# Pinning some weight loads to their place in the program on one DMA queue of a hybrid encoder block

## The chip, the cores and the metric

One core of a Trainium2 chip runs the whole kernel. Its engines are TensorE (PE in the profile, matmuls), VectorE (DVE, elementwise), ScalarE (ACT, elementwise and functions), GpSimd (POOL, elementwise) and SyncE (SP), which here does nothing but issue DMA transfers; each engine runs its own instructions in order and waits on semaphores for the others. The metric is the device time of one execution in microseconds, lower is better.

## The reference

A residual block on x of 512 frames by 1024 features, in float32:

```python
xn = rmsnorm(h, norm_mix_g[l])
u = jnp.einsum('bsd,de->bse', xn, w_in[l])
q, k, v, xr, gr, ga, gb = jnp.split(u, splits, axis=-1)
ya = chunked_band_attention(q, k, v, rel_table[l]) @ w_attn_out[l]      # 16 heads of 64
xc = causal_depthwise_conv(xr, conv_w[l], conv_b[l])
hr = rg_lru(xc, w_rg_r[l], b_rg_r[l], w_rg_i[l], b_rg_i[l], rg_lambda[l])
yb = (hr * jax.nn.gelu(gr)) @ w_rnn_out[l]
gates = jax.nn.sigmoid(jnp.concatenate([ga, gb], axis=-1) + b_merge[l])
g_a, g_b = jnp.split(gates, 2, axis=-1)
h = h + (g_a * ya + g_b * yb) @ w_o[l]
hn = rmsnorm(h, norm_ffn_g[l])
g, up = jnp.split(hn @ w_ffn_in[l], 2, axis=-1)
h = h + (jax.nn.silu(g) * up) @ w_ffn_out[l]
out = rmsnorm(h, final_norm_g)
```

## The kernel before

**Arithmetic.** Every product is made of three matmuls at reduced precision: both operands are split into a high part (ScalarE, line 82, rounds it) and a low part (VectorE, line 83, subtracts). A weight so split is a tile `whl_...`, from a loaded tile `raw_...` (line 143, issued by SP). For some large products (v, w_o, w_ffn_in, w_ffn_out) the kernel saves matmuls by Strassen-like sums of weight blocks. These sums of weights are made early, in time that VectorE has left over, and kept in DRAM: `spill` loads four blocks of 128 x 1024 (line 599, SP), makes four differences on VectorE (line 603), each in place, and stores each (lines 605 and 607, SP) into `sums...`, from where they are read much later. `spill_in` does the same for the first unit of w_ffn_in (loads at line 625, four operations at 628 to 632, stores at 635).

**Stages.** The recurrent branch comes first (xr, gr, gb; tiles u, gt, a, rnn), then the products `po_yb` of `rnn` with w_rnn_out, then v (`pv_mm`), then 16 attention heads, then the outputs, w_o and the FFN, which takes over half of the time.

**Where the loads stand in the program.**
- w_o: in the loop of the eight `po_yb` products, ahead of numbers 1 and 3, `spill_of(w_o, ...)` with four loads each (tiles `spillo0_n`, `spillo1_n`).
- w_ffn_out, unit 0 (tiles `spill_a2`, `spill_a3`, two loads each), and w_ffn_in (tiles `spill_fg2`, then `spill_fu2`, two loads each, in the same room): the generator `spills()`, which the loop of heads advances by one step ahead of each head from 2 on.

Around that loop a head h is worked thus: `transposed(h)` turns the probabilities `p` on TensorE (`pT`, line 744) and splits them (`pp`); `scores(h + 1)` makes `s` on TensorE from q, kh and kl (lines 725 and 726), the row maximum on VectorE (729), the exponential on ScalarE (730), the reciprocal `rl` of its sum on VectorE (731) and the normalisation on GpSimd (733); then come projections of q and k of a later pair of heads (`po_q`, `po_k`) and `weigh(h)` (`o`, line 764). q is copied out by ScalarE (678) and VectorE (679); kh and kl of a pair of heads by ScalarE (689, 691), VectorE (690) and GpSimd (692): kl of the odd head is GpSimd's copy of VectorE's difference.

**What sets the order.** On TensorE the program's order, by `manual_schedule`, in the heads and in the products of v. On SP, VectorE, ScalarE and GpSimd a scheduler orders the instructions of the program when the kernel is built, by its own model of when each can start, within their data dependencies and the room in the pools: so a load may be issued ahead of loads that stand in front of it in the program, and an operation on a loaded tile may stand ahead of others.

Of the kernel before, what the change touches and what calls it, by code (L numbers as in the profile page):

```python
# [14 lines left out]
P = 128  # L15
D = 1024
S = 512
# [15 lines left out]
CW = 256  # L33
# [3 lines left out]
def block_kernel(ctx: ExitStack, tc: tile.TileContext, x, norm_mix_g, w_in, b_merge, rel_table,  # L37
# [3 lines left out]
    pe, dve, act, pool, sp = nc.tensor, nc.vector, nc.scalar, nc.gpsimd, nc.sync  # L41
# [82 lines left out]
    units = (2, 3), (4, 5), (6, 7), (8, 9), (1, 10)  # L124
# [413 lines left out]
    def big(n, shape, dtype, name):  # L538
        return rnp.tile(shape, dtype, tag=f"big{n}", bufs=1, name=name)
# [42 lines left out]
    def drams(name):  # L582
        return [dr.tile([P, 2, S], F32, name=f"{name}_{n}") for n in range(4)]

    sums_d = [drams(f"sums{u}") for u in range(len(units))]
# [3 lines left out]
    def square(w, i, cc):  # L589
        rows = w[2 * P * i:2 * P * (i + 1), cc * S:(cc + 1) * S]  # L590
        return rows.rearrange("(k p) e -> p k e", p=P)
# [1 line left out]
    def fo_block(i, cc):  # L593
        return square(w_ffn_out, i, cc)

    def spill(w, unit, to, r):

        for n in range(4):
            sp.dma_start(out=r[n], in_=square(w, unit[n // 2], n % 2))
        b11, b12, b21, b22 = r  # L600
        for out_, i, a_, b_ in ((b11, 0, b12, b11), (b12, 2, b22, b12), (b22, 1, b22, b11), (b21, 3, b21, b22)):
            yield
            dve.tensor_sub(out_, a_, b_)
            if out_ is not b11:
                sp.dma_start(out=to[i][:], in_=out_)
            if out_ is b22:
                sp.dma_start(out=to[0][:], in_=b11)
# [5 lines left out]
    def spill_of(w, u, pl, tag, bufs):  # L613
        name, unit, to = {id(w_v): ("v", units_v, sums_v), id(w_o): ("o", units_o, sums_o)}.get(id(w), ("f", units, sums_d))
        r = [pl.tile([P, 2, S], F32, tag=tag, bufs=bufs, name=f"spill{name}{u}_{n}")[:] for n in range(4)]
        return spill(w, unit[u], to[u], r)

    first_sums = {f"f{w}2": [dr.tile([P, 2, 4, P], F32, name=f"sums_f{w}2_{n}") for n in range(2)] for w in "gu"}

    def spill_in(name, both):  # L620

        col = chunks[index[name]][1][0][1]
        r = [both[:, n] for n in range(2)]
        for n in range(2):
            sp.dma_start(out=r[n], in_=w_ffn_in[n * S:(n + 1) * S, col:col + CW].rearrange("(k p) e -> p k e", p=P))
        s2, s3, s4, s1 = (r[n][:, :, i * P:(i + 1) * P] for n in range(2) for i in range(2))
        yield
        dve.tensor_add(s1, s3, s1)
        dve.tensor_sub(s3, s2, s3)
        yield  # L630
        dve.tensor_sub(s2, s1, s2)
        dve.tensor_sub(s4, s4, s2)
        for to, of in zip(first_sums[name], ((s2, s1), (s3, s4))):
            for i in range(2):
                sp.dma_start(out=to[:, i], in_=of[i])
# [8 lines left out]
    for j in range(0, KT, 2):  # L644
        if j >= 4:
            at_once(spill_of(w_v, j // 2 - 2, early, "spill", 4))
        for c in range(2):
            conv[j + c] = rnn_conv(j + c, tile_of(f"xr{j}", c, ahead=2))
        for c in range(2):
            po = tile_of(f"gr{j}", c, "mm" if j == 0 else "t")  # L650
            conv[j + c] += (rnn_gelu(j + c, po),)
            gates_of(j + c)
        for c in range(2):
            gate(1, j + c)
# [221 lines left out]
    for j in range(KT):  # L876
        if j in (1, 3):
            at_once(spill_of(w_o, j // 2, aw, "v", 8))
        if j in (4, 5, 6, 7):
            xv_sum(("s1", "s2", "s4", "s3")[j - 4])  # L880
        if j == 6:
            blocks_v("b11")
        if j == 7:
            blocks_v("b21")
        po = mm_tile(f"po_yb{j}")
        project(po, weights(f"yb{j - j % 2}", 1 if j < 6 else 0), j % 2, rnn)
        dve.scalar_tensor_tensor(zB[j], zB[j], 1.0, po[:], ALU.add, ALU.mult)
# [37 lines left out]

    def spills():
        r = [big(n, [P, 2, 2, S], F32, f"spill_a{n}") for n in (2, 3)]
        yield from spill(w_ffn_out, units[0], sums_d[0], [r[n // 2][:, n % 2] for n in range(4)])
        yield from spill_in("fg2", big(2, [P, 2, 4, CW], F32, "spill_fg2"))
        yield from spill_in("fu2", big(3, [P, 2, 4, CW], F32, "spill_fu2"))  # L930

    spilling = spills()

    with tc.manual_schedule(engines={mybir.EngineType.PE}):
# [307 lines left out]
    def late():  # L1242
        for u in (1, 2, 3):
            yield from spill_of(w_ffn_out, u, acp, "act", 13)
# [26 lines left out]
    for j in range(2, FT, 2):  # L1271
# [6 lines left out]
        g, u = (sc.tile([P, 4, 256], F32, tag=f"c{w}", name=f"c_{w}{j}") for w in "gu")  # L1278
# [143 lines left out]
    with tc.manual_schedule(engines={mybir.EngineType.PE, mybir.EngineType.DVE, mybir.EngineType.Activation}):  # L1422
# [44 lines left out]
        x, w = acts["a22", last[0]], parts_w["t4", last[0]]  # L1467
# [39 lines left out]
```

## Time and profile before

| | us |
|---|---|
| median of 3 runs | 864.84 (864.70 to 865.08) |
| the profiled execution | 864.55 |
| its span, first to last instruction | 862.7 |
| TensorE busy | 845.0 (98%) |
| VectorE busy | 678.7 (79%) |
| ScalarE busy | 521.0 (60%) |
| GpSimd busy | 117.0 (14%) |
| mean granted TensorE clock | 0.995 of full speed |

Times in the profile's rows count from the first instruction. A row of a timeline gives start, duration, engine, line, operation, tiles (output<-inputs, numbers left out), shape, how many in a row, and in brackets how long the engine was idle before it and what released it. Engines with a q at the end (SPq) are the sequencers that issue transfers. The execution has 1.85 us around the span.

### The profile page before, as it was taken

The numbers are of one execution on the slowest core, as the hardware profiler recorded it, in microseconds if no ns is written. First come the engines' busy times: TensorE is split into PE (matmuls) and PEld (weight loads), VectorE is DVE, ScalarE is ACT, GpSimd is POOL, SyncE is SP. The second block draws the span as 40 slices with busy tenths as digits, with TensorE's granted clock in tenths as the row PEclk, the third lists the DMA queues.
The fourth block names the chain that finished last, engine by engine and source line by source line (L and its number), as shares of the span: only waits on it lengthen the run. The fifth ranks groups of instructions, "written<-read, shape, count | busy, mean of one in ns | idle before, by whom it ended". The sixth has DMA issues, their size and how long they took to land.

```text
span 862.7 us, 13109 instructions
## 1 busy us (share of the span) xinstructions
PE 845.0 (98%) x4860; PEld 738.7 (86%) x4860; DVE 678.7 (79%) x1006; ACT 521.0 (60%) x893; POOL 117.0 (14%) x152
## 2 busy tenths in 40 slices
PE   8999999999998999999999999999999999999997
PEld 6977887788886888888888889999999999988885
DVE  5789767797687777665568887988989887689985
ACT  7678677624565676766655456655565555385455
POOL 2324302220012433232200000000000001000002
PEclk9999999999998999999999999999999999999999
DMA  8694333953699422323247451565666242886622
GB/s 273 198 311 152 98 98 95 366 198 122 190 307 290 128 74 74 101 84 96 75 149 242 147 194 50 160 235 163 256 205 228 85 126 91 278 300 208 209 73 98
DMA packets 107599, 147.23 MB, mean 171 GB/s; under 512 B 7184, under 2 KB 77440, under 8 KB 107536
## 3 DMA queue, kind: packets, MB, share of 16 engines
q1 hardware_dynamic: 103856, 138.74, 48.9%
q10 hardware_dynamic: 3680, 7.67, 2.9%
q8 instruction: 38, 0.62, 0.3%
q14 instruction: 25, 0.20, 0.1%
HBM read 123.27 MB, written 23.11 MB: 170 GB/s over the span
## 4 chain that ended last, share of the span: by engine, by line
PE 85%; DVE 5%; DMA 3%; ACT 3%; POOL 2%; issue 1%; SPq 0%; ACTq 0%; DVEq 0%; POOLq 0%
PE po_out L76 4%; PE po_out L78 4%; PE po_out L77 4%; PE p_fu L76 2%; PE p_fg L78 2%; PE p_fu L78 2%; PE p_fu L77 2%; PE p_fg L76 2%; PE p_fg L77 2%; PE o L764 2%; PE po_ga L76 2%; PE po_ga L78 2%; PE po_ya L76 2%; PE po_ga L77 2%; PE po_ya L78 2%; PE po_ya L77 2%
## 5 line engine op out<-in xcount | busy, mean ns | idle before, releaser
L733 POOL TENSOR_SCALAR p<-p,rl 128x128 f32<-128x128 f32 (+1 forms) x64 | 41.6, 668 | 104.5 <-DVE rl L731 104.4
L730 ACT ACTIVATE p<-p,m 128x128 f32<-128x128 f32 (+1 forms) x64 | 35.8, 563 | 11.2 <-DVE m L729 11.2
L1219 POOL TENSOR_TENSOR act_lo<-act,act_hi 128x1024 fp32r<-128x1024 f32 x1 | 2.4, 2407 | 294.3 <-ACT act_hi L1218 294.3
L83 DVE TENSOR_TENSOR pp<-pT,pp 128x384 fp32r<-128x384 f32 (+1 forms) x48 | 28.0, 597 | 11.1 <-ACT pp L82 10.9
L83 DVE TENSOR_TENSOR whl_t<-raw_t,whl_t 128x1024 fp32r<-128x1024 f32 x26 | 32.1, 1236 | 0.3 <-ACT whl_t L82 0.3
L729 DVE CUSTOM_DVE_ANT_0 p<-s,bias 128x128 f32<-128x128 f32 (+1 forms) x64 | 29.0, 483 | 1.9 <-PE s L726 1.7
L76 PE MATMUL po_gr<-xnT,whl_gr 128*128 128x512 f32 (+1 forms) x80 | 28.2, 354 | 0.1
L82 ACT ACTIVATE whl_t<-raw_t 128x1024 fp32r<-128x1024 f32 x26 | 27.2, 1047 | 1.5 <-PE po_h L78 1.5
L77 PE MATMUL po_xr<-xnT,whl_xr 128*128 128x512 f32 (+1 forms) x80 | 27.8, 353 | 0.1
L77 PE MATMUL po_gr<-xnT,whl_gr 128*128 128x512 f32 (+1 forms) x80 | 27.6, 346 | 0.0
L78 PE MATMUL po_gr<-xnT,whl_gr 128*128 128x512 f32 (+1 forms) x80 | 27.5, 348 | 0.0
L78 PE MATMUL po_xr<-xnT,whl_xr 128*128 128x512 f32 (+1 forms) x80 | 27.3, 346 | 0.0
L76 PE MATMUL po_xr<-xnT,whl_xr 128*128 128x512 f32 (+1 forms) x80 | 26.7, 352 | 0.6 <-ACT xnT L358 0.6
L83 DVE TENSOR_TENSOR whl_fg_s<-s_fg,whl_fg_s 128x1024 fp32r<-128x1024 f32 x20 | 24.4, 1223 | 2.9 <-ACT whl_fg_s L82 2.9
L83 DVE TENSOR_TENSOR whl_fu_s<-s_fu,whl_fu_s 128x1024 fp32r<-128x1024 f32 x20 | 24.4, 1223 | 2.9 <-ACT whl_fu_s L82 2.9
L77 PE MATMUL po_yb<-rnn,whl_yb 128*128 128x512 f32 x64 | 25.1, 392 | 1.2 <-POOL rnn L549 1.2
L83 DVE TENSOR_TENSOR whl_qk<-raw_qk,whl_qk 128x1024 fp32r<-128x1024 f32 x16 | 21.1, 1321 | 5.9 <-ACT whl_qk L82 5.9
L76 PE MATMUL po_q<-xnT,whl_qk 128*128 128x512 f32 x64 | 25.6, 400 | 0.0
L76 PE MATMUL po_gb<-xnT,whl_gb 128*128 128x512 f32 x64 | 25.3, 395 | 0.2 <-DVE xc L497 0.2
L78 PE MATMUL po_q<-xnT,whl_qk 128*128 128x512 f32 x64 | 25.4, 397 | 0.0
L77 PE MATMUL po_q<-xnT,whl_qk 128*128 128x512 f32 x64 | 25.4, 396 | 0.0
L76 PE MATMUL po_ga<-xnT,whl_ga 128*128 128x512 f32 x64 | 25.4, 396 | 0.0
(472 smaller groups left out, 3300.6 us busy)
## 6 DMA issues: line engine op xcount, KB each, us to landing
raw_fg<-in_w_ffn_in_dram SPq DMA_DIRECT2D x22, 512.0 KB, 4.1
raw_fu<-in_w_ffn_in_dram SPq DMA_DIRECT2D x22, 512.0 KB, 3.6
raw_t<-sums SPq DMA_DIRECT2D x20, 512.0 KB, 4.0
raw_qk<-in_w_in_dram SPq DMA_DIRECT2D x32, 256.0 KB, 5.0
raw_b<-in_w_ffn_out_dram SPq DMA_DIRECT2D x15, 512.0 KB, 5.8
spillf<-in_w_ffn_out_dram SPq DMA_DIRECT2D x12, 512.0 KB, 8.2
sums<-spillf SPq DMA_DIRECT2D x12, 512.0 KB, 3.4
raw_xr<-in_w_in_dram SPq DMA_DIRECT2D x8, 512.0 KB, 4.6
```

What stands on the lines that cost most here:

```text
L76: pe.matmul(o, sh, mh, start=start, stop=False, skip_group_check=parts)
L77: pe.matmul(o, sh, ml, start=False, stop=False, skip_group_check=parts)
L78: pe.matmul(o, sl, mh, start=False, stop=stop, skip_group_check=parts)
L82: act.activation(hi, src, AF.Copy)
L83: dve.tensor_sub(lo, src, f(hi))
L729: dve.tensor_tensor_reduce(prob[qb][:], scs[qb], bias[:, S - w:S], -1.0, 3e38, ALU.add, ALU.min, nmax[:, qb:qb + 1])
L730: act.activation(prob[qb][:], prob[qb][:], AF.Exp, bias=nmax[:, qb:qb + 1], scale=-1.0, accum_out=lsum[:, qb:qb + 1])
L733: pool.tensor_scalar(prob[qb][:], prob[qb][:], rl[:, qb:qb + 1], 1.0, ALU.mult, ALU.mult)
L764: pe.matmul(po[:, S - n:S], st, pp[i][:, part, lo:lo + n], start=kb == 0 and part == 0, stop=kb == NT - 1 and part == 1)
L1219: pool.tensor_sub(lo[:], o[:], f(hi[:]))
```

## The change

`tc.keep_in_program_order(ins)` tells the scheduler that this instruction is issued no earlier than the one which stands just in front of it in the program on the same engine. It adds no instruction and no semaphore. It is put on the eight loads of w_o, the four of w_ffn_out's unit 0, and the four of `spill_in`; all are on SP. The loads of w_v and of the later units of w_ffn_out go through the same function and stay as they were.

```diff
+    def in_order(ins, pinned):
+        if pinned:
+            tc.keep_in_program_order(ins)
+
-    def spill(w, unit, to, r):
+    def spill(w, unit, to, r, pinned=False):
 
         for n in range(4):
-            sp.dma_start(out=r[n], in_=square(w, unit[n // 2], n % 2))
+            in_order(sp.dma_start(out=r[n], in_=square(w, unit[n // 2], n % 2)), pinned)
...
-        return spill(w, unit[u], to[u], r)
+        return spill(w, unit[u], to[u], r, w is w_o)
...
         for n in range(2):
-            sp.dma_start(out=r[n], in_=w_ffn_in[n * S:(n + 1) * S, col:col + CW].rearrange("(k p) e -> p k e", p=P))
+            in_order(sp.dma_start(out=r[n], in_=w_ffn_in[n * S:(n + 1) * S, col:col + CW].rearrange("(k p) e -> p k e", p=P)), True)
...
-        yield from spill(w_ffn_out, units[0], sums_d[0], [r[n // 2][:, n % 2] for n in range(4)])
+        yield from spill(w_ffn_out, units[0], sums_d[0], [r[n // 2][:, n % 2] for n in range(4)], True)
```

TensorE's instructions stand in the same order as before. Those of SP, VectorE, ScalarE and, in a few places, GpSimd move, since the scheduler places everything else around the pinned loads. All lines from the new function on are four higher after the change (599 becomes 603, 603 becomes 607, 679 becomes 683, 690 becomes 694, 731 becomes 735), so the rows of after carry other line numbers.

SP's queue around the first loads of w_o, before:

```order
L143 DMA raw_yb0_0_1578<-in_w_rnn_out_dram 128x4x256
L143 DMA raw_yb0_4_1583<-in_w_rnn_out_dram 128x4x256
L599 DMA spillo0_0_1697<-in_w_o_dram 128x2x512
L143 DMA raw_yb2_0_1662<-in_w_rnn_out_dram 128x4x256
L599 DMA spillo0_1_1698<-in_w_o_dram 128x2x512
L599 DMA spillo0_2_1699<-in_w_o_dram 128x2x512
L599 DMA spillo0_3_1700<-in_w_o_dram 128x2x512
L599 DMA spillo1_0_1775<-in_w_o_dram 128x2x512
```

And after:

```order
L143 DMA raw_yb0_0_1578<-in_w_rnn_out_dram 128x4x256
L143 DMA raw_yb0_4_1583<-in_w_rnn_out_dram 128x4x256
L143 DMA raw_yb2_0_1662<-in_w_rnn_out_dram 128x4x256
L143 DMA raw_yb2_4_1667<-in_w_rnn_out_dram 128x4x256
L603 DMA spillo0_0_1697<-in_w_o_dram 128x2x512
L603 DMA spillo0_1_1698<-in_w_o_dram 128x2x512
L603 DMA spillo0_2_1699<-in_w_o_dram 128x2x512
L603 DMA spillo0_3_1700<-in_w_o_dram 128x2x512
L143 DMA raw_yb4_0_1740<-in_w_rnn_out_dram 128x4x256
```

The loads of w_rnn_out for products 2 and 3 (raw_yb2) now go ahead of the first four loads of w_o, and the second four go behind raw_yb4.

VectorE's queue at the same place, before (gt and u are the recurrence of rnn 6 and 7, line 543 its scan, 544 its last step; whl_yb is a weight's low part):

```order
L603 TENSOR_TENSOR spillo0_0_1697<-spillo0_1_1698,spillo0_0_1697 128x1024
L542 SCALAR_TENSOR_TENSOR gt6_1_1431<-gt6_1_1431,u6_1436 128x512
L542 SCALAR_TENSOR_TENSOR gt7_1_1485<-gt7_1_1485,u6_1436 128x512
L83 TENSOR_TENSOR whl_yb0_0_1580<-raw_yb0_0_1578,whl_yb0_0_1580 128x1024
L543 SCALAR_TENSOR_TENSOR u6_1436<-a6_1440,gt6_1_1431 128x512
L543 SCALAR_TENSOR_TENSOR u6_1436<-a7_1493,gt7_1_1485 128x512
L603 TENSOR_TENSOR spillo0_1_1698<-spillo0_3_1700,spillo0_1_1698 128x1024
L83 TENSOR_TENSOR whl_yb0_4_1585<-raw_yb0_4_1583,whl_yb0_4_1585 128x1024
L544 SCALAR_TENSOR_TENSOR u6_1436<-u6_1436,g6_1415 128x512
L544 SCALAR_TENSOR_TENSOR u6_1436<-u6_1436,g7_1469 128x512
```

And after:

```order
L542 SCALAR_TENSOR_TENSOR gt6_1_1431<-gt6_1_1431,u6_1436 128x512
L542 SCALAR_TENSOR_TENSOR gt7_1_1485<-gt7_1_1485,u6_1436 128x512
L543 SCALAR_TENSOR_TENSOR u6_1436<-a6_1440,gt6_1_1431 128x512
L83 TENSOR_TENSOR whl_yb0_0_1580<-raw_yb0_0_1578,whl_yb0_0_1580 128x1024
L543 SCALAR_TENSOR_TENSOR u6_1436<-a7_1493,gt7_1_1485 128x512
L544 SCALAR_TENSOR_TENSOR u6_1436<-u6_1436,g6_1415 128x512
L83 TENSOR_TENSOR whl_yb0_4_1585<-raw_yb0_4_1583,whl_yb0_4_1585 128x1024
L544 SCALAR_TENSOR_TENSOR u6_1436<-u6_1436,g7_1469 128x512
L683 SCALAR_TENSOR_TENSOR q0_1612<-po_q0_1577,q0_1612 64x512
L607 TENSOR_TENSOR spillo0_0_1697<-spillo0_1_1698,spillo0_0_1697 128x1024
```

Both differences of spillo that stood ahead of the recurrence's last step now stand behind it.

SP's queue in the first heads, before (raw_qk are the weights of q and k, spill_a the blocks of w_ffn_out, spill_fg those of w_ffn_in):

```order
L143 DMA raw_qk1_0_2249<-in_w_in_dram 128x4x128 x2
L599 DMA spill_a2_2551<-in_w_ffn_out_dram 128x2x512 x2
L143 DMA raw_qk1_4_2255<-in_w_in_dram 128x4x128 x2
L143 DMA raw_qk2_0_2351<-in_w_in_dram 128x4x128 x2
L599 DMA spill_a3_2552<-in_w_ffn_out_dram 128x2x512 x2
L607 DMA sums0_0_442<-spill_a2_2551 128x1024
L143 DMA raw_qk2_4_2357<-in_w_in_dram 128x4x128 x2
L143 DMA raw_qk3_0_2496<-in_w_in_dram 128x4x128 x2
L605 DMA sums0_2_444<-spill_a2_2551 128x1024
L143 DMA raw_qk3_4_2502<-in_w_in_dram 128x4x128 x2
L605 DMA sums0_1_443<-spill_a3_2552 128x1024
L625 DMA spill_fg2_2994<-in_w_ffn_in_dram 128x4x256 x2
```

And after:

```order
L143 DMA raw_qk2_4_2357<-in_w_in_dram 128x4x128 x2
L143 DMA raw_qk3_0_2496<-in_w_in_dram 128x4x128 x2
L143 DMA raw_qk3_4_2502<-in_w_in_dram 128x4x128 x2
L603 DMA spill_a2_2551<-in_w_ffn_out_dram 128x2x512 x2
L603 DMA spill_a3_2552<-in_w_ffn_out_dram 128x2x512 x2
L143 DMA raw_qk4_0_2718<-in_w_in_dram 128x4x128 x2
L611 DMA sums0_0_442<-spill_a2_2551 128x1024
L609 DMA sums0_2_444<-spill_a2_2551 128x1024
L609 DMA sums0_1_443<-spill_a3_2552 128x1024
L143 DMA raw_qk4_4_2724<-in_w_in_dram 128x4x128 x2
L609 DMA sums0_3_445<-spill_a3_2552 128x1024
L629 DMA spill_fg2_2994<-in_w_ffn_in_dram 128x4x256 x2
```

All four loads of spill_a go behind those of qk3; the loads of spill_fg go behind qk4, and those of spill_fu, which stood between qk4 and qk5 on SP, behind the first half of qk5.

VectorE's queue ahead of kl of heads 2 and 3 (kl1), before:

```order
L603 TENSOR_TENSOR spill_a3_2552<-spill_a3_2552 128x1024
L731 RECIPROCAL rl1_2321<-l1_2319 128x4
L679 SCALAR_TENSOR_TENSOR q1_2387<-po_q1_2350,q1_2387 64x512
L628 TENSOR_TENSOR spill_fg2_2994<-spill_fg2_2994 128x4x128
L83 TENSOR_TENSOR whl_qk3_0_2499<-raw_qk3_0_2496,whl_qk3_0_2499 128x1024
L679 SCALAR_TENSOR_TENSOR q1_2387<-po_q1_2350,q1_2387 64x512
L629 TENSOR_TENSOR spill_fg2_2994<-spill_fg2_2994 128x4x128
L690 TENSOR_TENSOR kl1_2418<-po_k1_2392,kh1_2417 64x512
L631 TENSOR_TENSOR spill_fg2_2994<-spill_fg2_2994 128x4x128
```

And after:

```order
L735 RECIPROCAL rl1_2321<-l1_2319 128x4
L607 TENSOR_TENSOR spill_a2_2551<-spill_a2_2551 128x1024
L683 SCALAR_TENSOR_TENSOR q1_2387<-po_q1_2350,q1_2387 64x512
L607 TENSOR_TENSOR spill_a2_2551<-spill_a3_2552,spill_a2_2551 128x1024
L683 SCALAR_TENSOR_TENSOR q1_2387<-po_q1_2350,q1_2387 64x512
L607 TENSOR_TENSOR spill_a3_2552<-spill_a3_2552,spill_a2_2551 128x1024
L83 TENSOR_TENSOR whl_qk3_0_2499<-raw_qk3_0_2496,whl_qk3_0_2499 128x1024
L607 TENSOR_TENSOR spill_a3_2552<-spill_a3_2552 128x1024
L694 TENSOR_TENSOR kl1_2418<-po_k1_2392,kh1_2417 64x512
```

The operations on spill_fg have left this stretch, and all four on spill_a stand in it; one of those stood ahead of rl of head 0 before, the others between the heads' first operations. The four on spill_fg now stand behind the maxima of head 2, around its reciprocal, and of those on spill_fu one stands just ahead of the reciprocal of head 3 and two ahead of kl of heads 4 and 5.

## The prediction

> **What bounds the kernel.** I read the page first (span, busy shares, granted clock), then TensorE's waits by releaser, then TensorE's busy time by stage, then the timelines of all engines around the two places at which the change moves instructions.
>
> ```profile
> span 862.7 us, 13109 instructions
> ...
> PE 845.0 (98%) x4860; PEld 738.7 (86%) x4860; DVE 678.7 (79%) x1006; ACT 521.0 (60%) x893; POOL 117.0 (14%) x152
> ...
> PEclk9999999999998999999999999999999999999999
> ```
>
> TensorE is the bound: 98% busy, at full clock but for one slice of 40. No edit here changes its work, so the change can give back only what it loses: idle time, and time at a low clock. The next two views show how much that is (stretch, busy time and matmuls, granted clock, DMA share, GB/s):
>
> ```profile
> 170.00:175.00 5.00, 3.76 (x16) 1.00 0.79 320
> 270.00:275.00 5.00, 2.67 (x8) 0.61 0.88 237
> 275.00:280.00 5.00, 5.00 (x17) 0.71 1.09 335
> ...
> 340.00:440.00 100.00, 100.00 (x521) 1.00 0.26 80
> 540.00:850.00 310.00, 309.98 (x2188) 1.00 0.55 184
> ```
>
> ```profile
> PE s L725 <- ACT kh L691: 4.0, 3, 3.1
> PE s L726 <- POOL kl L692: 1.5, 2, 1.1
> ...
> PE po_yb L77 <- POOL rnn L549: 1.2, 1, 1.2
> ...
> PE pT L744 <- POOL p L733: 0.9, 3, 0.3
> ```
>
> From 340 us on there is nothing to win. The waits that matter are at 172 us (po_yb), 252 us (pT of head 0) and 268 to 273 us (s of head 2), and after the last comes a spell at a low clock. Each lies just where loads are pinned. I sum against the profiled execution, 864.55 us (span 862.7 and 1.85 around it), which is 0.29 under the median of 864.84.
>
> **Term 1, the pinned loads of w_o.** At 172 us TensorE waits for the low part of rnn 6 and 7; the chain behind it:
>
> ```profile
> 158.20 1.23 DVE L603 TENSOR_TENSOR spillo<-spillo,spillo 128x1024 f32<-128x1024 f32 x1 [1.94 <-DMA spillo<-in_w_o_dram]
> ...
> 163.93 1.20 DVE L603 TENSOR_TENSOR spillo<-spillo,spillo 128x1024 f32<-128x1024 f32 x1
> ...
> 166.18 1.29 DVE L544 SCALAR_TENSOR_TENSOR u<-u,g 128x512 f32<-128x512 f32 x2
> 167.75 5.35 POOL L549 TENSOR_TENSOR rnn<-u,rnn 128x512 fp32r<-128x512 f32 x2 [12.00 <-ACT rnn L548]
> 173.16 0.50 PE L77 MATMUL po_yb<-rnn,whl_yb 128*128 128x512 f32 x1 [1.24 <-POOL rnn L549]
> ```
>
> DVE meets a subtraction of spillo before its load has landed (1.94 us), does it, does another, and only then the last step of the recurrence (L544); GpSimd follows. (Operations of 1.22 us follow each other every 1.15 on DVE, so 1.15 is what each costs in a row.) In the new order both subtractions stand behind L544, so L544 ends about 1.94 + 2 x 1.15 = 4.2 us earlier where nothing else holds it, or 3 us where ScalarE's part does. GpSimd's 5.35 us then ends near 169 to 170 against the 171.9 at which TensorE wants it. The wait goes. Bounds: 0 (GpSimd gets slower, next to the moved subtractions) and −1.24; I take **−1.2**, as the slack of 2 us is larger than any doubt in the rows. The raw_yb loads pass ahead of the spillo loads on SP's queue; that can only bring them earlier.
>
> **Term 2, the loads of w_ffn_out, first half.** DVE does a spill_a subtraction ahead of rl of head 0, and GpSimd's normalisation of p waits for rl:
>
> ```profile
> 245.39 1.23 DVE L603 TENSOR_TENSOR spill_a<-spill_a 128x1024 f32<-128x1024 f32 x1 [0.58 <-DMA spill_a<-in_w_ffn_out_dram]
> ...
> 248.87 0.18 DVE L731 RECIPROCAL rl<-l 128x4 f32<-128x4 f32 x1
> ...
> 249.33 3.27 POOL L733 TENSOR_SCALAR p<-p,rl 128x128 f32<-128x128 f32 x4
> 251.99 0.33 PE L744 MATMUL pT<-ident,p 128*128 128x128 f32 x1 [0.23 <-POOL p L733]
> 252.66 0.98 PE L744 MATMUL pT<-ident,p 128*128 128x128 f32 x7 [0.34 <-POOL p L733]
> ```
>
> Without it rl comes 0.58 + 1.15 = 1.7 us earlier, TensorE only 1.2 earlier (term 1): the 0.23 and 0.34 shrink by up to 0.5. Bounds 0 and −0.57; I take **−0.5**. Late next there would be the memory clear and load of the bias tile, which GpSimd does in the same place.
>
> **Term 3, the stall of head 2.** The rows of DVE, GpSimd and TensorE:
>
> ```profile
> 252.50 1.22 DVE L603 TENSOR_TENSOR spill_a<-spill_a,spill_a 128x1024 f32<-128x1024 f32 x1 [1.15 <-DMA spill_a<-in_w_ffn_out_dram]
> 253.64 1.22 DVE L83 TENSOR_TENSOR whl_qk<-raw_qk,whl_qk 128x1024 fp32r<-128x1024 f32 x1
> ...
> 266.56 0.69 DVE L628 TENSOR_TENSOR spill_fg<-spill_fg 128x512 f32<-128x512 f32 x1 [3.72 <-DMA raw_qk<-in_w_in_dram]
> ...
> 269.87 0.68 DVE L690 TENSOR_TENSOR kl<-po_k,kh 64x512 fp32r<-64x512 f32 x1
> 270.61 2.14 POOL L692 CAST kl<-kl 64x512 fp32r<-64x512 f32 x1 [4.47 <-DVE kl L690]
> ...
> 266.87 1.28 PE L744 MATMUL pT<-ident,p 128*128 128x128 f32 x10
> 271.22 0.48 PE L725 MATMUL s<-kh,q 128*128 128x128 f32 x1 [3.07 <-ACT kh L691]
> 272.81 0.47 PE L726 MATMUL s<-kl,q 128*128 128x128 f32 x1 [1.11 <-POOL kl L692]
> ```
>
> DVE stands 3.72 us in front of the spill_fg addition (the row names raw_qk, which that operation doesn't read; what it needs is the load of spill_fg), and kl of heads 2 and 3 is queued behind it. In the new order spill_fg is gone from here, but all four spill_a subtractions (two done earlier before, two now added) stand between rl of head 1 and kl. So the stall isn't removed, it becomes a shorter one, which I build up. The spill_a loads go out behind raw_qk3, whose buffer is free when the split of whl_qk2 ends: 253.64 + 1.22 = 254.86 before, and without the 1.15 + 1.15 in front of it and with TensorE 1.2 us earlier about 251.4. Behind two loads of raw_qk3 the four follow at about 252.3 to 253.6, by the 0.44 us that SP needs for each:
>
> ```profile
> 245.98 0.88 SPq L599 DMA_DIRECT2D spill_a<-in_w_ffn_out_dram  x2
> ```
>
> How long they take, by the issues' median time to landing (the last column):
>
> ```profile
> spillo<-in_w_o_dram SPq DMA_DIRECT2D x8, 512.0 KB, 9.0
> ...
> spill_fg<-in_w_ffn_in_dram SPq DMA_DIRECT2D x2, 512.0 KB, 5.1
> ...
> spill_fu<-in_w_ffn_in_dram SPq DMA_DIRECT2D x2, 512.0 KB, 7.1
> ```
>
> These are 5.1 to 9.0 us for loads of this size; the nearest in time and crowd is spill_fu with 7.1, so the last lands near 260.7 (258.7 to 262.6). The second subtraction reads it. From there DVE does three subtractions, a q half, a whl_qk half and the first kl: 3 x 1.15 + 0.6 + 1.15 + 0.68 = 5.9 us, so kl ends near 266.5. ScalarE's kh waits for that kl, and GpSimd's copy runs beside DVE's next whl_qk half: up to 2.14 us, to about 268.4. TensorE, by then 1.7 us earlier, wants kl at 266.87 + 1.28 − 1.7 = 266.4. The stall is about 2.0 where it was 3.07 + 1.11 = 4.18. Bounds: 1.7 left (the loads early, ScalarE and GpSimd last) to 4.3 left (9.0 us to landing). I take **−2.1**.
>
> **Term 4, the clock.** From 270 to 280 us the granted clock is 0.61 and 0.71, so 0.39 x 5 + 0.29 x 5 = 3.4 us of full clock are missing; some 1 us of it falls in the idle time itself, the rest, 2.4, lengthened matmuls. The 1.24 us of idle at 172 left the clock at 1.00, 4.2 us with one matmul in between took it down. A stall of 2.0 is nearer to the first. Bounds 0 and −2.5; I take **−2.3**.
>
> The Trainium skill, "TensorE: Matmul & The Clock Gate", section "Part 1: The HAM clock gate", says the clock halves after an idle window of about 3.4 us; this trace agrees (0.61 in the stretch with the 4.2 us). By that rule a stall of 2.0 or even 3 us keeps the term whole; by the rows alone, which show nothing between 1.24 and 4.2, it could be lost at 2.0 already, and the sum would be −2.8.
>
> **Term 5, what the later loads push.** spill_fg and spill_fu move from heads 1 and 2 into heads 2 to 4: a spill_fu addition now stands just ahead of rl of head 3 and two more ahead of kl of heads 4 and 5, where TensorE has no slack:
>
> ```profile
> 277.42 0.08 DVE L729 DVE_READ_ACCUMULATOR2_ANT m<- 128x1 f32 x1
> ...
> 288.69 0.55 DVE L83 TENSOR_TENSOR pp<-pT,pp 128x384 fp32r<-128x384 f32 x1
> 289.71 0.18 DVE L731 RECIPROCAL rl<-l 128x4 f32<-128x4 f32 x1 [0.47 <-ACT p L730]
> ...
> 294.70 0.33 PE L726 MATMUL s<-kl,q 128*128 128x128 f32 x1 [0.37 <-POOL kl L692]
> ...
> 278.49 0.69 DVE L628 TENSOR_TENSOR spill_fu<-spill_fu 128x512 f32<-128x512 f32 x1 [0.98 <-DMA raw_qk<-in_w_in_dram]
> ```
>
> One addition (0.6) partly fits in DVE's idle 0.47; two more (1.2) go straight into kl. Whether the first waits for its load: terms 1 to 4 bring DVE 6.1 us earlier here, so the last maximum of head 2 ends at 277.50 − 6.1 = 271.4, four spill_fg operations and rl take 2.7 more, and behind their stores on SP the two loads are issued up to about 275.6. With 7.1 us the later one lands at 282.7; DVE comes to its reader at 289.24 − 6.1 = 283.1. So it is just in time, and with 9.0 us 1.5 late. Bounds 0 and +2.8 (0.6 + 1.2 less 0.5, and 1.5); I take **+1.0**, nearer to the first, since the wait is unlikely and part of the 1.3 is hidden by GpSimd's own work. The sums that these loads feed are read much later, and TensorE shows no wait for them anywhere; that the w_o sums are stored a few us later costs nothing for the same reason.
>
> **Sum.** −1.2 − 0.5 − 2.1 − 2.3 + 1.0 = −5.1: 864.55 − 5.1 = 859.45, and 859.7 against the median.
>
> **Rivals.** 0.2% is 1.7 us, about what this measurement can tell from no change: faster means under 863.1, slower over 866.6.
>
> (a) *The new wait takes the place of the old.* spill_a's last load takes 9.0 us, as spillo's did, lands at 262.6, kl ends at 268.5, GpSimd at 270.6: 4.2 us of stall and the low clock with it. Left are terms 1, 2 and 5: −0.7, 864.1. For it speaks that the loads meet raw_qk3 and the bias in the queues; against it, that spill_fg and spill_fu, in the same crowd, took 5.1 and 7.1.
>
> (b) *All of it goes:* loads at 5.1 us, stall 1.7, spell gone, nothing new at head 4: −1.24 − 0.57 − 2.5 − 2.5 = −6.8, and less again if head 4's own 0.7 of waits goes: 857.3 to 858.0.
>
> (c) *Slower.* The spill_fu addition ahead of rl of head 3 waits for its load. All that GpSimd does for head 3 stands behind rl, and TensorE's transposes behind that. At 11.9 us from issue to landing DVE is held 4.4 us, which also takes the clock down (2.4): −5.1 + 6.8 = +1.7, 866.5; later than that it is slower. For: the DMA share there was 1.09 of all engines at 275 to 280. Against: no group above shows a median over 9.0.
>
> (d) *No effect*, because other work would wait equally at both stalls: against it, DVE's instructions in front of both change, and the releasers named are DVE's.
>
> The Trainium skill, "DMA: Bandwidth & Descriptors", section "Rules for kernel authors", advises to issue a load early and wait for it late; this change issues spill_a's second pair some 7 us later (245.98 to 253), with its readers near behind. By that rule (a) or (c) would be the outcome. The trace is against it so far: here the early loads were read too early as well, by DVE's order.
>
> **How the numbers follow.** Forecast 0.68, (a) 0.13 (most of it within 0.2%, a little faster), (b) 0.10, (c) 0.07, (d) 0.02. Faster 0.81, same 0.12, slower 0.07. The time is the forecast's, 859.7. The range reaches from a little past (b), 857.0, to 863.5, near (a): with stalls between 2.0 and 4.2 and the spell in part it fills up to there.
>
> **What the profile after would show.** Right: no wait of po_yb for rnn near 172; pT of head 0 without waits; a wait of s of head 2 of about 2 us, released by kh or kl, with the granted clock at 1.00 from 260 to 280; DVE's 3.72 us gone and a wait for spill_a in its place; s of head 4 waiting a us more. Wrong: a stall at head 2 of 3.5 us or more, a slice of low clock, or a DVE wait for spill_fu of over 2 us.

## The result, and the profile after

The changed kernel takes 869.94 us (median of 4, 868.76 to 870.58) against 864.96 before: a ratio of 1.0053, interval 1.0036 to 1.0071. It is slower, by 5 us; the forecast was 859.7, 5 us faster, in a range that ended at 863.5. The profiled execution took 870.58 us. Its page, with the lines shown before:

```profile
span 868.6 us, 13104 instructions
...
PE 847.8 (98%) x4860; PEld 740.7 (85%) x4860; DVE 676.7 (78%) x1006; ACT 520.7 (60%) x893; POOL 116.7 (13%) x152
...
PEclk9999999999998899999999999999999999999999
```

TensorE is busy 2.8 us longer with the same 4860 matmuls, so part of the loss is clock, and two slices are dimmed instead of one. Its waits by releaser (us in total, times, longest):

```profile
PE s L729 <- ACT kh L695: 7.9, 4, 5.9
PE pT L748 <- POOL p L737: 3.5, 5, 2.1
...
PE s L730 <- POOL kl L696: 0.5, 1, 0.5
```

The wait of po_yb is gone from the list, as forecast. But s of head 2 waits 5.9 us for kh and 0.5 for kl where it waited 3.1 and 1.1, and pT waits 3.5 us in all instead of 0.9. By stage (stretch, busy, granted clock, DMA share, GB/s):

```profile
260.00:270.00 10.00, 5.32 (x32) 0.98 0.73 271
270.00:280.00 10.00, 8.25 (x28) 0.68 0.90 284
280.00:290.00 10.00, 9.19 (x50) 1.00 0.72 222
290.00:300.00 10.00, 6.22 (x32) 0.85 0.77 229
300.00:305.00 5.00, 5.00 (x16) 0.62 0.17 52
```

Since TensorE runs the same matmuls in the same order in all kernels, the start of the same matmul in two traces says where time went. Shifts against before, in us (minus is earlier), from the two start times:

| first matmul of | start before | after |
|---|---|---|
| v's products | 211.82 | −1.90 |
| s of head 1 | 253.40 | −2.83 |
| s of head 2 | 271.22 | +0.02 |
| pT of head 2 | 283.10 | −0.98 |
| pT of head 3 | 292.18 | +0.27 |
| s of head 4 | 294.00 | +4.17 |
| s of head 5 | 303.69 | +6.17 |
| FFN | 547.84 | +6.22 |

Terms 1 and 2 came (−2.83, of which −0.26 is there at 144 us already). All of that and more was lost in two places: in front of s of head 2 (2.85 us, of which 1.0 came back: 0.6 since the wait for kl behind it is 0.51 us instead of 1.11, and 0.4 in clock) and from pT of head 2 to pT of head 4 (7.2 us).

**Head 2.** VectorE's, GpSimd's and TensorE's rows:

```profile
261.54 1.23 DVE L607 TENSOR_TENSOR spill_a<-spill_a 128x1024 f32<-128x1024 f32 x1 [5.65 <-DMA spill_a<-in_w_ffn_out_dram]
...
264.37 1.23 DVE L607 TENSOR_TENSOR spill_a<-spill_a,spill_a 128x1024 f32<-128x1024 f32 x1 [0.90 <-DMA spill_a<-in_w_ffn_out_dram]
...
269.88 0.68 DVE L694 TENSOR_TENSOR kl<-po_k,kh 64x512 fp32r<-64x512 f32 x1
270.63 1.54 POOL L696 CAST kl<-kl 64x512 fp32r<-64x512 f32 x1 [8.31 <-DVE kl L694]
...
271.24 0.47 PE L729 MATMUL s<-kh,q 128*128 128x128 f32 x1 [5.92 <-ACT kh L695]
272.23 0.47 PE L730 MATMUL s<-kl,q 128*128 128x128 f32 x1 [0.51 <-POOL kl L696]
```

The wait for spill_fg (3.72 us) has become a wait for spill_a (5.65 + 0.90). kl starts at 269.88, to a hundredth where it started before, though TensorE now wants it 2.8 us sooner. How the loads went (the issues of line 603 with first and last start, and their time to landing, which the trace has for two of the four):

```profile
L603 SPq DMA_DIRECT2D spill_a<-in_w_ffn_out_dram x4: 408/458/461, 251.9 to 253.4; - x4
...
DMA to landing us min/median/max: 9.1/9.5/10.0
```

They were issued when the prediction said (252.3 to 253.6), but took 9.5 us in the middle, not 7.1; the operation that needs the last started 10.9 us after its issue. The DMA engines were full all that time (busy time of TensorE, its weight loads, VectorE, ScalarE and GpSimd, then the granted clock, the share of the 16 DMA engines and GB/s):

```profile
252.50:255.00 2.50, 2.50 (x13) 2.05 (x12) 2.50 (x7) 1.61 (x7) 0.00 (x0) 1.00 1.08 269
255.00:257.50 2.50, 2.50 (x13) 2.07 (x12) 0.88 (x3) 0.67 (x2) 1.52 (x4) 1.00 0.93 272
257.50:260.00 2.50, 2.50 (x13) 2.07 (x12) 0.00 (x0) 0.59 (x1) 0.53 (x1) 1.00 1.05 356
260.00:262.50 2.50, 2.50 (x13) 2.07 (x12) 0.96 (x1) 0.00 (x0) 0.15 (x1) 1.00 1.03 347
```

**Heads 2 to 4.** The operations on spill_fg and spill_fu stand ahead of reciprocals and kl:

```profile
279.42 0.69 DVE L632 TENSOR_TENSOR spill_fg<-spill_fg 128x512 f32<-128x512 f32 x1 [3.10 <-issue]
...
290.32 5.73 POOL L737 TENSOR_SCALAR p<-p,rl 128x128 f32<-128x128 f32 x4 [6.49 <-DVE rl L735]
...
295.43 0.33 PE L748 MATMUL pT<-ident,p 128*128 128x128 f32 x1 [2.11 <-POOL p L737]
...
298.17 0.47 PE L729 MATMUL s<-kh,q 128*128 128x128 f32 x1 [1.07 <-ACT kh L695]
```

VectorE idles 3.10 us ahead of the first one, and rl of head 2 stands behind it; the row names no releaser, but what that operation lacks is its load, issued at 270.4 and 270.8. And GpSimd's normalisation of head 3 took 5.73 us, in which VectorE did three operations on spill_fu and two whl_qk halves (before, with a whl_qk half beside it, 3.02). TensorE waited for both, and the clock went down again (0.85, 0.62).

### The profile page after: what moved, and what is told of

Same layout as the page of the kernel before. It is cut to its first block, busy times and chain, and to the rows that moved or that the text cites. A ratio compares the mean times of both kernels' runs of the same rounds, so it can differ in the third digit from the quotient of the medians.

```text
span 868.6 us, 13104 instructions
## 1 busy us (share of the span) xinstructions
PE 847.8 (98%) x4860; PEld 740.7 (85%) x4860; DVE 676.7 (78%) x1006; ACT 520.7 (60%) x893; POOL 116.7 (13%) x152
## 4 chain that ended last, share of the span: by engine, by line
PE 92%; DMA 3%; ACT 2%; DVE 1%; issue 1%; POOL 1%; SPq 0%; ACTq 0%; POOLq 0%; DVEq 0%
PE po_out L76 4%; PE po_out L77 4%; PE po_out L78 4%; PE p_fu L78 2%; PE p_fg L78 2%; PE p_fu L76 2%; PE p_fg L76 2%; PE p_fg L77 2%; PE p_fu L77 2%; PE o L768 2%; PE po_gb L76 2%; PE po_gb L77 2%; PE po_ga L76 2%; PE po_ga L78 2%; PE po_ya L76 2%; PE po_gb L78 2%
## 5 line engine op out<-in xcount | busy, mean ns | idle before, releaser
L737 POOL TENSOR_SCALAR p<-p,rl 128x128 f32<-128x128 f32 (+1 forms) x64 | 44.6, 714 | 104.1 <-DVE rl L735 104.0
L729 PE MATMUL s<-kh,q 128*128 128x128 f32 (+1 forms) x64 | 22.1, 366 | 7.9 <-ACT kh L695 7.9
L82 ACT ACTIVATE whl_fu_s<-s_fu 128x1024 fp32r<-128x1024 f32 x20 | 21.0, 1056 | 7.8 <-PE q_fu L78 2.6
L748 PE MATMUL pT<-ident,p 128*128 128x128 f32 x160 | 21.9, 277 | 3.6 <-POOL p L737 3.5
```

Of the source, the lines that this page charges most:

```text
L82: act.activation(hi, src, AF.Copy)
L729: pe.matmul(scs[qb], qs, kh[:, e, 0:w], start=True, stop=False)
L737: pool.tensor_scalar(prob[qb][:], prob[qb][:], rl[:, qb:qb + 1], 1.0, ALU.mult, ALU.mult)
L748: pe.transpose(pt[:, at * P:(at + 1) * P], prob[qb][:, kb * P:(kb + 1) * P], ident[:])
```

## The experiments

Times are medians with the ratio to before on the same chip and its interval. Shifts as above:

| kernel | us | ratio | v's products | s of head 1 | s of head 2 | pT of head 2 | s of head 4 | s of head 9 |
|---|---|---|---|---|---|---|---|---|
| after | 869.94 | 1.0053 | −1.90 | −2.83 | +0.02 | −0.98 | +4.17 | +6.20 |
| 1: w_o alone | 863.00 | 0.9979 | −1.79 | −2.47 | −1.66 | −2.53 | −1.78 | −2.37 |
| 2: spill_a alone | 870.67 | 1.0067 | −0.06 | −0.99 | +1.17 | +0.40 | +4.60 | +5.55 |
| 3: w_ffn_in alone | 862.56 | 0.9975 | −0.08 | −0.76 | −3.28 | −5.87 | −1.50 | −1.43 |
| 4: operations pinned too | 858.73 | 0.9928 | −1.97 | −2.89 | −5.42 | −9.24 | −9.25 | −4.75 |
| 5: operations, not loads | 860.75 | 0.9949 | −1.66 | −2.57 | −5.11 | −8.93 | −8.96 | −3.62 |
| 6: w_ffn_in's operations | 862.60 | 0.9969 | −0.79 | −1.71 | −0.16 | −1.33 | −1.37 | −1.93 |
| 7: step behind the scores | 857.85 | 0.9909 | −0.49 | −1.42 | −3.96 | −7.78 | −7.79 | −6.17 |
| 8: step behind q or k | 864.54 | 0.9994 | −1.54 | −2.47 | −5.01 | −8.83 | −8.84 | +0.25 |
| 9: half of spill_a's bytes | 866.04 | 1.0014 | −1.66 | −2.57 | −4.02 | −4.88 | −0.28 | +0.66 |

Shifts of a few tenths, and in 6 and 7 of some 1 us, are there before 144 us already; differences between columns are what counts. The experiments ran on two chips, whose medians of before differ by up to 0.8 us, so times are compared by their ratios.

**1 to 3: one part of the change each.** 1: only w_o pinned.

```diff
-        yield from spill(w_ffn_out, units[0], sums_d[0], [...], True)
+        yield from spill(w_ffn_out, units[0], sums_d[0], [...])
-            in_order(sp.dma_start(out=r[n], in_=w_ffn_in[...]), True)
+            in_order(sp.dma_start(out=r[n], in_=w_ffn_in[...]), False)
```

> Only the loads of w_o are pinned; the heads are ordered as before. Theory A (each part of the change acts at its own place; what VectorE has queued in front of the recurrence's last step and of kl decides): po_yb no longer waits near 172 us, TensorE enters the heads 1.6 us earlier, as it did after the change, and the stall of head 2 stays at about 4.2 us with its low clock: 864.9 - 1.6 = 863.3. Rival B (the heads' loads land when the queue lets them, whenever TensorE arrives): the stall of head 2 grows by what was won, 864.9.

863.00 (0.9970 to 0.9989): theory A. 1.6 us are won ahead of v. At head 2, 0.8 of the 2.5 us won by then are lost again, which is a part of rival B, and come back in clock. Between v and s of head 1 another 0.68 us are won, though the operation on spill_a stands ahead of rl of head 0 as before; it no longer waits 0.58 us for its load there:

```profile
242.93 1.22 DVE L607 TENSOR_TENSOR spill_a<-spill_a 128x1024 f32<-128x1024 f32 x1
```

2: only spill_a pinned.

```diff
-        return spill(w, unit[u], to[u], r, w is w_o)
+        return spill(w, unit[u], to[u], r)
-            in_order(sp.dma_start(out=r[n], in_=w_ffn_in[...]), True)
+            in_order(sp.dma_start(out=r[n], in_=w_ffn_in[...]), False)
```

> Only the loads of w_ffn_out's unit 0 (spill_a) are pinned. VectorE's order in heads 0 to 2 is that of the changed kernel, and at heads 2 to 4 nearly so, though spill_fg and spill_fu aren't pinned, because they use the room that spill_a leaves later. Theory A: VectorE waits over 5 us for spill_a ahead of kl, TensorE stands some 6 us at head 2, and heads 3 and 4 lose about as much as in the changed kernel: 864.9 + 6.6 = 871.5, the worst of the four. Rival B (the pinned loads of w_ffn_in are the larger harm, by being late themselves): 866 to 868.

870.67 (1.0044 to 1.0090): theory A. This part alone does as much harm as the whole change; w_ffn_in comes late without being pinned, since it loads into spill_a's room.

3: only w_ffn_in pinned.

```diff
-        return spill(w, unit[u], to[u], r, w is w_o)
+        return spill(w, unit[u], to[u], r)
-        yield from spill(w_ffn_out, units[0], sums_d[0], [...], True)
+        yield from spill(w_ffn_out, units[0], sums_d[0], [...])
```

> Only the loads of w_ffn_in (spill_fg, spill_fu) are pinned; spill_a as before. VectorE has no spill operation between rl of head 1 and kl any more. Theory A: the stall of head 2 falls from 4.2 us to under 2 and the clock stays up (about -4.5), and the additions of spill_fg ahead of rl of head 2 and of spill_fu ahead of rl of head 3 and of kl take some of it back (+1 to +4): 861.5 to 864.5. Rival B (what moved to heads 3 and 4 costs as much as in the changed kernel, 7 us with its own low clock): 867.

862.56 (0.9965 to 0.9985): theory A. Head 2 is passed 2.5 us sooner and the clock stays up (−5.87 at pT of head 2), and heads 2 to 4 take 4.4 us of it back, without a stall at head 2 ahead of them. GpSimd's normalisation of head 3 is as long as in the changed kernel:

```profile
285.31 5.73 POOL L737 TENSOR_SCALAR p<-p,rl 128x128 f32<-128x128 f32 x4 [6.24 <-DVE rl L735]
```

**4: the operations pinned too.** The loads stay as in the changed kernel.

```diff
-            dve.tensor_sub(out_, a_, b_)
+            in_order(dve.tensor_sub(out_, a_, b_), to is sums_d[0])
...
-        dve.tensor_add(s1, s3, s1)
+        in_order(dve.tensor_add(s1, s3, s1), True)
```

(and the three others of `spill_in`).

> As the changed kernel, and the operations of VectorE on spill_a, spill_fg and spill_fu are pinned to their place in the program as well (they come one head after another, from head 3 on, each long after its load). Nothing is left out. Theory A (the loads' lateness harms only because VectorE reads them at once, ahead of kl and rl): no wait of VectorE for a spill load, head 2 stalls under 1 us, no low clock, 1.6 + 0.9 + 4 + 2.5 less than before, and something back where the operations stand now: 856 to 858. Rival B (the crowd of transfers itself delays raw_qk, bias and the rest): stalls of some us stay in heads 1 to 4, over 862.

858.73 (0.9907 to 0.9949). The loads were issued and landed as late as in the changed kernel, and it cost nothing:

```profile
DMA to landing us min/median/max: 8.8/9.3/9.9
```

VectorE's row of kl of heads 2 and 3, and TensorE's stretch there:

```profile
263.60 0.68 DVE L694 TENSOR_TENSOR kl<-po_k,kh 64x512 fp32r<-64x512 f32 x1 [0.98 <-ACT kh L693]
```

```profile
260.00:270.00 10.00, 9.46 (x52) 1.00 0.71 217
```

kl starts at 263.60 instead of 269.88, and TensorE is 9.25 us ahead of before at head 4. So it is VectorE's order, not the loads' lateness and not the crowd of transfers in itself (rival B: over 862). Heads 5 to 8, where the scheduler put the pinned operations ahead of some reciprocals, take 4.5 us back, so the time is a little over theory A's 856 to 858. What that looks like at head 7, by the us:

```profile
323.00:324.00 1.00, 0.77 (x6) 1.00 0.92 226
324.00:325.00 1.00, 0.18 (x1) 1.00 1.01 330
325.00:326.00 1.00, 0.51 (x5) 1.00 1.08 377
326.00:327.00 1.00, 1.00 (x8) 0.53 1.10 363
327.00:328.00 1.00, 1.00 (x5) 0.50 1.15 346
328.00:329.00 1.00, 1.00 (x4) 0.50 1.10 382
```

Three us with 1.5 us of idle in pieces, and the clock is halved for the next three.

**5: the operations without the loads.** As 4, with 1's edit besides: the loads in the heads are free and issued as early as before, w_o's are pinned.

> w_o's loads pinned, and in the heads VectorE's operations on spill_a, spill_fg and spill_fu pinned to their place in the program, but the loads of spill_a, spill_fg and spill_fu free, so that the scheduler issues spill_a's as early as before the change. Nothing is left out. Theory A (only what VectorE has queued in front of kl and rl counts, not when the loads go out): the same as with the loads pinned too, 858.7, give or take 0.8. Rival C (early loads stand in the queue ahead of raw_qk and delay it, so that pinning the loads is worth something for itself): 860 to 862, with waits for raw_qk in heads 0 to 2.

860.75 (0.9934 to 0.9964), outside theory A's 858.7 ± 0.8, though by the ratios the interval overlaps that of 4. It isn't rival C, which looked for waits in heads 0 to 2: up to s of head 5 this kernel runs as 4 does (−8.32 against −8.65 there). What differs comes at heads 7 and 8, where VectorE's order differs too (spill_fg's first addition, ready sooner, stands ahead of a half of kl); whether that is all of the 1.1 us between the two traces was not tried. In the stretch at issue, up to s of head 5, the time of the loads is worth nothing once they are read late.

**6: only w_ffn_in's operations pinned.** As the changed kernel, with the second half of 4's edit (the four operations of `spill_in`).

> As the changed kernel, with VectorE's operations on spill_fg and spill_fu alone pinned to their place in the program (from head 8 on); those on spill_a stay in front of kl of heads 2 and 3. Nothing is left out. Theory A: head 2 stalls over 6 us and has its low clock as in the changed kernel, so TensorE leaves it 1 us earlier than before the change; heads 3 and 4 lose nothing; some 1 to 2 us go to the later places: 864 to 866. Rival D (the loss at heads 3 and 4 comes from the stall at head 2 and the crowd of transfers behind it, not from the operations on spill_fg and spill_fu): 868 to 870.

862.60 (0.9956 to 0.9982). Head 2 and GpSimd at head 3:

```profile
271.06 0.48 PE L729 MATMUL s<-kh,q 128*128 128x128 f32 x1 [4.62 <-ACT kh L695]
...
288.19 3.03 POOL L737 TENSOR_SCALAR p<-p,rl 128x128 f32<-128x128 f32 x4 [8.19 <-DVE rl L735]
```

The stall of head 2 stays (4.62 + 0.51, TensorE being 1.1 us later from the start), and between pT of head 2 and s of head 4 nothing is lost, where the changed kernel loses 5.2: GpSimd is back at 3.03 us. Rival D falls, here as in experiment 3: the loss at heads 2 to 4 is those operations. It ended better than theory A's 864 to 866, since their later places cost almost nothing (−1.37 at head 4, −1.93 at head 9).

**7 and 8: other places for the step.** As 4, with the step moved behind the next scores (7):

```diff
-            if h > 1:
-                next(spilling, None)
             pp = transposed(h, prob)
             if h + 1 < HEADS:
                 prob = scores(h + 1)
+            if h > 1:
+                next(spilling, None)
             before, after = laid[h].split("|")
             project_all(before)
```

> Loads and VectorE's operations pinned, and the step of the spilling stands behind the scores of the next head instead of at the head's start, so that each operation follows a reciprocal, where VectorE is idle for some us until q or kl. Nothing is left out. Theory A: no spill operation in front of rl or kl, so the waits that the fourth experiment still had at heads 5 to 8 go, apart from GpSimd's normalisation, which runs beside the operation: 855 to 858. Rival E (GpSimd is held up by each operation of VectorE in the same us, 2.05 becomes 3 us or more, and pT waits for it at ten heads): 859 to 862.

857.85 (0.9893 to 0.9926): theory A, and the lowest time of all; its interval overlaps that of 4, so that it is faster than 4 isn't shown by the times. GpSimd is held up, as rival E has it, but for head 5, for instance, at no cost to TensorE, whose shift is −7.55 at s of heads 5 and 6 alike:

```profile
300.76 0.17 DVE L735 RECIPROCAL rl<-l 128x4 f32<-128x4 f32 x1
300.85 1.20 DVE L607 TENSOR_TENSOR spill_a<-spill_a,spill_a 128x1024 f32<-128x1024 f32 x1
...
301.13 3.89 POOL L737 TENSOR_SCALAR p<-p,rl 128x128 f32<-128x128 f32 x4 [5.57 <-DVE rl L735]
```

In 8 the same two lines stand behind `project_all(before)`.

> As the one before, but the step stands behind the projections of q or k, so that each operation follows the last half of q or kl and stands ahead of the next head's maxima. Nothing is left out. Theory A: nothing of kl or rl waits for a load, each operation delays the maxima and with them rl by up to 1.2 us, which the odd heads (kl) cannot hide: 856.5 to 859.5. Rival E (only GpSimd's overlap counts, and here GpSimd is idle but for the copy of kl): 854.5 to 856.5.

864.54 (0.9985 to 1.0003): neither theory. Ahead of the maxima each operation makes rl late, and the scheduler put a half of whl_qk ahead of rl as well:

```profile
295.48 1.23 DVE L607 TENSOR_TENSOR spill_a<-spill_a 128x1024 f32<-128x1024 f32 x1
...
300.52 1.22 DVE L83 TENSOR_TENSOR whl_qk<-raw_qk,whl_qk 128x1024 fp32r<-128x1024 f32 x1
301.66 0.17 DVE L735 RECIPROCAL rl<-l 128x4 f32<-128x4 f32 x1
...
303.09 2.95 POOL L737 TENSOR_SCALAR p<-p,rl 128x128 f32<-128x128 f32 x4
...
304.42 0.78 PE L748 MATMUL pT<-ident,p 128*128 128x128 f32 x2 [1.92 <-POOL p L737]
```

From −8.84 at head 4 it falls to +0.25 at head 9: from there on 9 us are lost here and 1.6 in 7, by the operations' place and by what the scheduler moved around it.

**9: half of the bytes.** As the changed kernel, with two of spill_a's four loads left out.

```diff
-        for n in range(4):
+        for n in (0, 2) if to is sums_d[0] else range(4):
...
+        if to is sums_d[0]:
+            r = [r[0], r[0][:], r[2], r[2][:]]
```

> As the changed kernel, but only two of the four blocks of w_ffn_out's unit 0 are loaded (1 MB in place of 2), and the four differences are made from these two; the sums of unit 0 that the FFN reads are therefore others than the reference's, in the same number and size. VectorE has the four operations in front of kl as in the changed kernel, one of them ahead of rl of head 1 and the last behind the first half of kl. Theory F (the loads land late because four of them stand in a row in the DMA engines, at some 350 GB/s): with 1 MB less the last lands 3 to 4 us earlier, near 260.5, VectorE waits 2 us or less for it, the stall of head 2 is 2 to 3.5 us in place of 6.4, heads 3 and 4 lose as in the changed kernel: 865 to 867.5. Rival G (a load from w_ffn_out takes 8 to 11 us here by itself): the last lands at 262 to 264, the stall stays over 5 us, 868 to 870.

866.04 (1.0003 to 1.0025): theory F. The time to landing of the two loads, then rows of VectorE and TensorE and TensorE's stretch (busy, clock, DMA share, GB/s):

```profile
DMA to landing us min/median/max: 7.6/7.6/7.6
```

```profile
258.90 1.23 DVE L609 TENSOR_TENSOR spill_a<-spill_a 128x1024 f32<-128x1024 f32 x1 [2.89 <-DMA spill_a<-in_w_ffn_out_dram]
260.36 1.23 DVE L609 TENSOR_TENSOR spill_a<-spill_a,spill_a 128x1024 f32<-128x1024 f32 x1
...
265.84 0.68 DVE L696 TENSOR_TENSOR kl<-po_k,kh 64x512 fp32r<-64x512 f32 x1
...
267.20 0.33 PE L731 MATMUL s<-kh,q 128*128 128x128 f32 x1 [1.63 <-ACT kh L697]
...
270.06 0.80 PE L76 MATMUL po_q<-xnT,whl_qk 128*128 128x512 f32 x1 [1.32 <-DVE oacc L772]
```

```profile
270.00:275.00 5.00, 4.93 (x16) 0.70 1.04 313
```

The second operation, which needs the last load, starts at 260.36 instead of 264.37, and kl as much sooner, at 265.84: VectorE's order isn't quite the same (rl of head 1 stands behind the first operation, and the fourth behind the first half of kl instead of ahead of it), but from the second operation to kl it takes 5.5 us as before. The stall at s is 1.63 us, and 1.32 us more follow in front of po_q; the clock goes down behind them (0.70). Heads 2 to 4 then lose 4.6 us up to s of head 4 (−4.88 to −0.28), against 5.2 in the changed kernel. So the bytes in line make a large part of the loads' time to landing: without 1 MB of them, 4 us at their reader.

## Why the prediction was wrong, point by point

- **Terms 1 and 2** (−1.2 and −0.5): right in direction, and a little small; both gains lie past the bounds (1.24 and 0.57). TensorE gained 1.64 at po_yb and 0.93 at pT of head 0. Experiment 1 shows the first, 2 the second. The reason given for the second was only in part right: in experiments 1 and 3 the operation still stands ahead of rl and 0.68 of the 0.93 came as well, since it no longer waited for its load. So its own 1.15 us, moved away, are worth some 0.25.
- **Term 3** (−2.1, bounds 1.7 to 4.3 us of stall): the step that failed first. The chain behind the last load was right: from 264.37 to kl's start at 269.88 there are 5.5 us, forecast 5.2. The landing was wrong. I took the median time of a pair of loads in another place, 7.1 us, and 9.0 as the upper end, and didn't count what stood in the line: two loads of raw_qk (256 KB each), four of 512 KB, two more of raw_qk and the bias, over 3 MB issued in 4 us. At the 269 to 356 GB/s that the engines moved here that is, by my estimate, 9 to 12 us of work. Both bounds were medians of other bursts, so neither was a bound. Experiment 9 bears it out by halving spill_a's bytes. The last load's reader started at 264.37, where I had the landing at 260.7, and TensorE, 2.8 us early instead of 1.7, wanted kl 1.1 us sooner than I had reckoned. The stall was 6.4 us (5.92 and 0.51), against 2.0 forecast and 4.18 before, beyond rival (a), whose mechanism it is.
- **Term 4** (−2.3): with the stall it had to fail; 0.4 came. Its size was right: in experiment 4, whose clock stays up there, 2.4 us were won in clock at head 2. But the criterion was wrong as well: I held a stall of 2.0 us for harmless. In experiment 9, waits of 1.63 and 1.32 us brought the clock down, and in experiment 4, at head 7, 1.5 us of idle in pieces within 3 us did. The Trainium skill, "TensorE: Matmul & The Clock Gate", section "Part 1: The HAM clock gate", gives an idle window of about 3.4 us; in experiment 4 the low spell lasted about that long, but less idle time set it off, and pT's short matmuls between the pieces didn't prevent it.
- **Term 5** (+1.0, bounds 0 and +2.8): the largest error; 7.2 us came, some 2 of them in clock. I looked at spill_fu's load only, and didn't price the first spill_fg operation ahead of rl of head 2, which stood 3.10 us for its load (1.26 us on TensorE). And "part of the 1.3 is hidden by GpSimd's own work" had it the wrong way round: GpSimd's normalisation got longer, 5.73 us, while VectorE did those operations. The profile before had that, in the normalisations of head 3, with a whl_qk half of VectorE beside it, and of head 4, with none:

```profile
290.09 3.02 POOL L733 TENSOR_SCALAR p<-p,rl 128x128 f32<-128x128 f32 x4 [6.90 <-DVE rl L731]
300.11 2.05 POOL L733 TENSOR_SCALAR p<-p,rl 128x128 f32<-128x128 f32 x4 [3.93 <-DVE rl L731]
```

  Experiment 6 takes the operations away and with them the loss.
- **The rivals:** (a) and (c) were priced one at a time; both places failed together, and (a)'s price lacked the longer stall (4.2 us for 6.4). (c) named head 3 and a late load as its cause; it was GpSimd's slowness and the spill_fg load.
- **The Trainium skill's rule** on early loads ("DMA: Bandwidth & Descriptors", section "Rules for kernel authors") pointed the right way, and experiments 4 and 5 show which half of it counts here: with the reading put late, loads of both times gave the same up to head 4 (−9.25 and −8.96).

## What to carry to other kernels

Price a moved load by the bytes that are in line around it on the DMA engines, not by the landing time of another load. Where a scheduler orders the engines, pinning a load moves what reads it too: look where each reader now stands, and if it stands ahead of something that TensorE waits for, pin the reader as well; here that turned 5 us lost into some 6 to 7.5 us won (experiments 4 and 7). In an in-order engine's queue, work that nobody waits for belongs behind the last thing somebody waits for, and best where the engine idles next.

## What the runs showed of the hardware

- Four normalisations on GpSimd took 2.05 us alone, 2.8 to 3.1 with one operation of 128 x 1024 between SBUF tiles on VectorE beside them, 3.89 with two, and 5.73 with three of spill_fu's and two whl_qk halves.
- With many loads in a row the DMA engines moved 269 to 356 GB/s at shares of 0.93 to 1.08; the last of four 512 KB loads was read 10.9 us after its issue as soon as it came, the last of two had come 7.7 us after (260.36 against 252.7).
- TensorE's clock was halved for some 3 us after 3 us in which it was idle for 1.5 in pieces (experiment 4), and was at 0.70 over the 5 us behind waits of 1.63 and 1.32 us (experiment 9); 1.24 us of idle among long matmuls, at 172 us before the change, left it up.
